# Down projection of a two-layer decoder trunk: 12 instead of 8 of 22 row tiles by seven products

## The chip, the cores and the metric

One core of a Trainium2 chip runs the whole program in one launch. The metric is the device time of that launch in microseconds; the host only lays arrays out. The kernel is written in Bass with the Tile framework: Tile assigns buffers, places semaphores and orders the instructions of every engine but PE, whose order is that of the program text.

Names of the engines as the profile has them: PE multiplies matrices (PEld is its loading of the stationary operand), DVE is the vector engine, ACT the scalar engine, POOL is GpSimd, which here only issues transfers, and SP issues the others.

## What is computed

The reference is two layers of a decoder trunk over 512 tokens of width 1024 in float32. Each layer has a gated feed-forward block, a mixer (a gated recurrence beside windowed attention) and a second gated feed-forward block, each between two normalisations. The change touches the feed-forward blocks alone:

```python
def swiglu(h, w_gate, w_up, w_down):
    return (jax.nn.silu(h @ w_gate) * (h @ w_up)) @ w_down

x = x + 0.5 * rms_norm(swiglu(h, w_ffn1_gate[l], w_ffn1_up[l], w_ffn1_down[l]), gn[1])
```

The inner width is 2816, so the down projection `... @ w_down` multiplies 512 x 2816 by 2816 x 1024. It is run four times: twice per layer, in two layers.

## The kernel before

**Precision.** Every float32 factor is split into hi (rounded to the format fp32r) and lo (the rest), and a product is three passes, hi x hi, hi x lo and lo x hi (`mm3`). A split is an ACT copy that makes hi and a DVE subtraction that makes lo (`split`, L401 and L402 for activations; L325 and L332, or L282 and L287, for weights). `split_dma` makes lo in another way: ACT makes hi (L411), ACT writes the negative of the source (L412), and a transfer issued by POOL adds the source to it (L413); DVE has no part in it.

**Tiles of the down projection.** The activations lie as 22 row tiles of 128 inner indices by 512 tokens, the list `src`. Each is the stationary operand, 128 tokens at a time; a half of the weight's columns (512) is the moving one. The result is `y[t][h]` in PSUM, for four token tiles t and two column halves h. A unit (j, h) is the pair of row tiles 2j and 2j + 1 for one column half; its weights are one item of 128 x 1024, and `both(j, h)` runs its 24 matmuls.

**Seven products.** For eight row tiles (8 to 15, `LEAD` = 8 and the next eight) the 2 x 2 block product of (two halves of the tokens, two groups of four rows) with (two groups of four rows, two column halves) is done in Winograd's form by seven instead of eight block products. `Late.sums` prepares the sums of the activations: x1 (the first block as it is), s for products 5 and 6, and t for products 3 and 7. `Stream.quarter` prepares those of the weights, of raw units and of `side` loads b12 and b22 that stay in SBUF. `quarters` runs the products in the order `ORDER` = p1, p6, p2, p7, p5, p4, p3, two weight items each, and adds them up on DVE (L790).

**Order of one projection before.** Four lead units of half 0 (rows 0 to 7), during which `Late.sums` runs for one row per unit and `ready` splits the rows `EARLY` = 4 ahead; then the seven products; then the units 8, 9 and 10 of half 0; `fetch` (the residual and the gains, to SBUF); three units of half 1; and the tail, the last four units of half 1 (`TAIL`), run one token tile after the other, with the normalisation of a finished token tile (`post`, `norm`) beside the matmuls of the next. The first block of the next stage is started in the tail (`pre.turn`). Ahead of the projection lies the loop of `sevenths`, one per row tile; the last one's silu and z (L895, L896) make row 21.

**Buffers and queues.** Nearly all activations of 128 x 512 share the tag "s" with 61 slots; a slot is taken by the first instruction that writes the tile and is free after the last one that uses it. Raw weight units have 4 slots (`W32`), hi and lo of weights 6 each (`WS`), and weight items are prepared `AHEAD` = 3 (`most`) items ahead of the one in use. "tt" has two slots, "m" one. `pin` keeps an instruction behind the one written before it on its engine; without it Tile may move an instruction forward when its inputs and its slot are there. PSUM has five tiles "acc" and three "aux". SP issues the loads in its order, POOL the adding transfers in its own.

Of the kernel before, what the change touches and what calls it, by code (L numbers as in the profile page):

```python
# [15 lines left out]
P = 128  # L16
# [22 lines left out]
LEAD = 8  # L39
ORDER = ("p1", "p6", "p2", "p7", "p5", "p4", "p3")  # L40
DMAS = ()
# [4 lines left out]
def trunk(ctx: ExitStack, tc: tile.TileContext, xin, wall, gains, lbT, hgain, sinks, c_dist, c_mask, c_ident, out):  # L46
# [109 lines left out]
    class Stream:  # L156
# [36 lines left out]
        def rows(self, kt, fast):  # L193
# [13 lines left out]

            j0, later = LEAD // 2 if fast else 0, []
            if fast:
                for j in range(j0):  # L210
                    unit(j, 0)

                u = self.n
                for q in range(2):
                    self.src[u + q] = pieces(j0 + q, 0)
                    self.src[u + 2 + q] = pieces(j0 + 2 + q, 0)
                self.side[u + 1] = [pieces(j0 + q, 1) for q in range(4)]
                for k in ORDER:
                    for q in range(2):
# [3 lines left out]
                self.t2 = [None, None]  # L223
                self.n += 4
                for j in range(j0):
                    later.append(j)
                j0 += 4
            for j in range(j0, kt // 2):
                unit(j, 0)
                later.append(j)  # L230
            for j in later:
                unit(j, 1)
            self.wall = u0 + kt

        def load(self, upto):
            while self.dma < min(upto, self.n):
# [10 lines left out]
                if u in self.side:  # L247
                    self.b12, self.b22 = [], []
                    for i, ps in enumerate(self.side[u]):
                        v = [big(), big()]  # L250
                        for c, a in ps:
                            nc.sync.dma_start(v[c.start // S][:, c.start % S : c.start % S + 2 * P], a)
                        (self.b22 if i > 1 else self.b12).append(v)

        def quarter(self, it):

            self.load(it.base + 4)
            q, h = it.q, (slice(0, S), slice(S, D))
            if it.kind in ("p1", "p2", "p5", "p4"):
                w = [self.raw[it.u][:, c] for c in h]  # L260
                if it.kind == "p4":
                    for c in range(2):
                        pin(nc.vector.tensor_tensor(w[c], w[c], self.t2[q][c], op=ALU.add))
            elif it.kind == "p6":

                t = sb.tile([P, D], F32, tag="tt", name=nm("tt"), bufs=2)
                self.t2[q] = w = [t[:, c] for c in h]
                for c in range(2):
                    t1 = self.raw[it.u][:, h[c]]
                    pin(nc.vector.tensor_tensor(t1, t1, self.b12[q][c], op=ALU.subtract))  # L270
                    pin(nc.vector.tensor_tensor(w[c], t1, self.b22[q][c], op=ALU.subtract))
            elif it.kind == "p3":
                w = self.b22[q]
            elif it.kind == "p7":

                w = self.b12[q]
                for c in range(2):
                    pin(nc.vector.tensor_tensor(w[c], w[c], self.b22[q][c], op=ALU.add))
            it.hi = sb.tile([P, D], F32R, tag="whi", name=nm("whi"), bufs=WS)
            it.lo = sb.tile([P, D], F32R, tag="wlo", name=nm("wlo"), bufs=WS)  # L280
            for c in range(2):
                nc.scalar.copy(it.hi[:, h[c]], w[c])  # L282
                if it.kind in DMAS:
                    nc.scalar.mul(it.lo[:, h[c]], w[c], -1.0)
                    nc.gpsimd.dma_start(it.lo[:, h[c]].bitcast(F32), w[c], accum_op=ALU.add)
                else:
                    nc.vector.tensor_tensor(it.lo[:, h[c]], w[c], it.hi[:, h[c]].bitcast(F32), op=ALU.subtract)  # L287
            self.done += 1
            self.flight += 1
            if it.kind in ("p5", "p4"):  # L290
                self.raw.pop(it.u)
                self.freed += 1
                self.load(self.freed + W32)
# [103 lines left out]
    def split(src, scale=None, to=None):  # L397

        hi, lo = to or (big(F32R), big(F32R))
        if scale is None:  # L400
            nc.scalar.copy(hi, src)  # L401
# [70 lines left out]
    class Quarters:  # L472
# [4 lines left out]
        def operand(self, n):  # L477
# [4 lines left out]
            return [[v[:, i, :] for v in x[k]] for k in range(4)]  # L482
# [127 lines left out]
    class Late(Quarters):  # L610


        def __init__(self, src, k0):
            self.src, self.k0 = src, k0
            self.x1, self.x56, self.x37, self.t = [], [], [], []
# [12 lines left out]
        def more(self, n):  # L628

            for i in range(len(self.x37), n):  # L630
                self.src[self.k0 + 4 + i] = split(self.src[self.k0 + 4 + i])
                self.x37.append(pair_split(self.t[i], split_dma))

        def raw(self, half, i):
            return [cut(self.src[self.k0 + 4 + k], HALF[half]) for k in range(4)] if i else self.x1

    def down(src, kt, l, n, nxt, fast):
# [8 lines left out]
        pre = Pre(*nxt) if nxt else None  # L646

        def ready(n):

            for i in range(min(n, kt)):  # L650
# [6 lines left out]
        def piece(b, t, h, j, i):  # L657
            st = cut(src[2 * j + i], slice(t * P, (t + 1) * P))
            mm3(y[t][h], st, [halves(w, i) for w in b[2:]], 2 * j + i == 0 and not (fast and h and t < 2), 2 * j + i == kt - 1)
# [20 lines left out]
        js = list(range(kt // 2))  # L680
        if fast:
            late = Late(src, LEAD)
            for j in range(LEAD // 2):
                ready(2 * j + EARLY)
                while len(late.x56) < min(4, 8 * (j + 1) / LEAD):
                    late.sums()
                both(j, 0)
            more = quarters(late, y)
            del js[LEAD // 2 : LEAD // 2 + 4]
        for j in js[LEAD // 2 if fast else 0 :]:  # L690
            ready(2 * j + 2 + EARLY)
            both(j, 0)
        if not fast:
            for t in range(TT):
                y[t][1] = aux() if t > 1 else acc()
        fetch()
        last = js[-TAIL:]
        for j in js[:-TAIL]:
            both(j, 1)

        warm = small([P, 1], "warm", 2)
        pin(nc.scalar.activation(out=warm, in_=src[last[0]][0][:, :1].bitcast(F32), func=AF.Sqrt, bias=eps_t, scale=0.0))
# [69 lines left out]
    def quarters(late, y):  # L772
# [3 lines left out]
        def product(n, o, start, stop=True):  # L776
            its = [ws.whole(), ws.whole()]
            for k in range(4):
                for t in range(2):
                    st = cut(late.operand(n)[k], slice(t * P, (t + 1) * P))  # L780
                    it = its[k // 2]
                    mv = [w.rearrange("p (m two c) -> p m two c", two=2, c=P)[:, :, k % 2, :] for w in (it.hi, it.lo)]
                    mm3(o[t], st, mv, start and k == 0, stop and k == 3)
# [12 lines left out]
        late.more(2)  # L796
        p = product(1, two(acc), True)
        p1, u2, u3, c12, c22 = (two(big) for _ in range(5))
        for t in range(2):
            nc.scalar.copy(p1[t], p[t])  # L800
        late.more(4)

# [649 lines left out]
```

## Time and profile before

| | before |
|---|---|
| median of 3 runs | 2100.99 us (2100.95 to 2102.06) |
| the profiled execution: its own time | 2100.66 us |
| the profiled execution: span | 2098.9 us |
| first matmul of the four fast down projections, in the span | 240.9, 935.1, 1279.3, 1973.2 us |

The page of the profile has the busy time of each engine and its share of the span first, then the span in 40 slices, then the chain of work that ended last by engine. A group line reads: line of the kernel, engine, operation, tiles out<-in, shape, count, then busy us and mean ns of one, then the idle time of the engine just before these instructions and what ended it. A line of the chain or of an engine's instructions in order of time reads: start in us, us, what, count. A line of windows reads: stretch, its length, busy us (and instructions) of PE, PEld, DVE, ACT and POOL, the granted clock, the busy share of the DMA engines, GB/s. Times that are given "after a lead's start" count from the first matmul of a down projection.

### The profile page before, as it was taken

Reading aid. Unit: us, or ns where it says so; the run is one execution under the profiler, and the core shown is the slowest. Engines: PE = TensorE matmul, PEld = TensorE weight load, DVE = VectorE, ACT = ScalarE, POOL = GpSimd, SP = SyncE. Lnnn points to the kernel's source line nnn. Section 1 sums busy time; section 2 is a strip of 40 time slices with the busy share of each in tenths; the row PEclk is TensorE's granted clock in tenths of the full one; section 3 lists DMA queues with packets and bytes.
Section 4 is the critical chain, followed back from the end, with each engine's and each line's share of the span. In section 5 each row is a group of like instructions: output and inputs, shape, how many; then the busy total and the mean of one; then the engine's idle time right before and its main releaser. Section 6 shows DMA issues by size and latency. Waiting matters only on the chain.

```text
span 2098.9 us, 35207 instructions
## 1 busy us (share of the span) xinstructions
PE 2090.3 (100%) x13549; PEld 1875.3 (89%) x13549; DVE 1550.5 (74%) x2705; ACT 1122.4 (53%) x1899; POOL 154.2 (7%) x188
## 2 busy tenths in 40 slices
PE   9999999999999999999999999999999999999998
PEld 8899988887888999998899998898778989999987
DVE  5877886766776777789587778767687758777884
ACT  6555564456454555556455556554653545555562
POOL 0011000000000011110001110000000000111000
PEclk9999999999999999999999999999999999999999
DMA  8577653312236357774447775632122563677651
GB/s 246 152 181 184 178 157 135 111 61 71 71 101 203 127 122 182 181 198 122 154 114 176 183 181 150 191 120 92 51 81 61 136 193 103 159 182 181 184 160 51
DMA packets 148071, 298.35 MB, mean 142 GB/s; under 512 B 16992, under 2 KB 74816, under 8 KB 147904
## 3 DMA queue, kind: packets, MB, share of 16 engines
q1 hardware_dynamic: 122416, 228.16, 33.2%
q0 software_dynamic: 25344, 67.91, 18.7%
q8 instruction: 106, 1.74, 0.3%
q14 instruction: 61, 0.50, 0.1%
q10 hardware_dynamic: 144, 0.05, 0.0%
HBM read 213.43 MB, written 14.73 MB: 109 GB/s over the span
## 4 chain that ended last, share of the span: by engine, by line
PE 88%; DMA 0%; DVE 0%; ACT 0%; SPq 0%; issue 0%; ACTq 0%
PE acc L115 64%; PE aux L115 22%; PE aux L125 1%; PE acc L125 1%; DMA wlo<-w 0%; DMA w<-wall 0%; SPq L241 0%; DVE s L402 0%; ACT whi L282 0%; DVE s L731 0%; ACT s L600 0%; DVE s L712 0%; DVE s L896 0%; DVE wlo L287 0%; ACT m L895 0%
## 5 line engine op out<-in xcount | busy, mean ns | idle before, releaser
L115 PE MATMUL acc<-s,whi 128*128 128x256 f32 (+1 forms) x4952 | 1059.3, 311 | 0.4 <-ACT whi L325 0.3
L115 PEld LDWEIGHTS acc<-s,whi 128*128 128x128 f32 x4952 | 808.0, 191 | 51.3 <-issue 3.2
L115 PE MATMUL acc<-s,wlo 128*128 128x256 f32 (+1 forms) x2476 | 766.6, 310 | 0.1
L115 PEld LDWEIGHTS acc<-s,wlo 128*128 128x128 f32 x2476 | 472.6, 191 | 25.0 <-DVE wlo L332 0.4
L325 ACT CAST whi<-w 128x1024 fp32r<-128x1024 f32 (+1 forms) x341 | 316.6, 948 | 237.6 <-PE acc L115 95.5
L115 PE MATMUL acc<-whi,s 128*128 128x512 f32 x1264 | 413.6, 393 | 0.1
L325 ACT CAST whi<-tt 128x1024 fp32r<-128x1024 f32 x154 | 161.4, 1048 | 326.5 <-DVE tt L319 184.2
L332 DVE TENSOR_TENSOR wlo<-w,whi 128x1024 fp32r<-128x1024 f32 (+1 forms) x181 | 218.3, 1215 | 151.4 <-ACT whi L325 149.6
L115 PEld LDWEIGHTS acc<-whi,s 128*128 128x128 f32 x1264 | 237.1, 188 | 54.7 <-ACT whi L325 1.6
L332 DVE TENSOR_TENSOR wlo<-tt,whi 128x1024 fp32r<-128x1024 f32 x154 | 188.1, 1221 | 98.8 <-ACT whi L325 98.7
L115 PE MATMUL acc<-wlo,s 128*128 128x512 f32 x632 | 246.4, 390 | 0.0
L115 PE MATMUL aux<-s,whi 128*128 128x256 f32 (+1 forms) x1248 | 230.4, 285 | 0.0
L330 POOL DMA_DIRECT2D wlo<-w x160 | 137.8, 863 | 1258.6 <-ACT wlo L329 704.9
L115 PE MATMUL aux<-whi,s 128*128 128x512 f32 x592 | 196.7, 390 | 0.0
L115 PEld LDWEIGHTS aux<-s,whi 128*128 128x128 f32 x1248 | 195.2, 192 | 1.1 <-issue 0.5
L115 PE MATMUL aux<-s,wlo 128*128 128x256 f32 (+1 forms) x624 | 177.5, 284 | 0.0
L115 PEld LDWEIGHTS acc<-wlo,s 128*128 128x128 f32 x632 | 118.7, 188 | 23.4
L115 PEld LDWEIGHTS aux<-whi,s 128*128 128x128 f32 x592 | 111.1, 188 | 22.8
L329 ACT ACTIVATE wlo<-w 128x1024 fp32r<-128x1024 f32 (+1 forms) x160 | 129.8, 844 | 0.0
L401 ACT CAST s<-s 128x512 fp32r<-128x512 f32 (+1 forms) x164 | 88.4, 580 | 71.5 <-DVE s L460 67.9
L115 PEld LDWEIGHTS aux<-s,wlo 128*128 128x128 f32 x624 | 119.8, 192 | 0.3
L115 PE MATMUL aux<-wlo,s 128*128 128x512 f32 x296 | 115.2, 389 | 0.0
(186 smaller groups left out, 2128.6 us busy)
## 6 DMA issues: line engine op xcount, KB each, us to landing
w<-wall SPq DMA_DIRECT2D x267, 512.0 KB, 3.7
wlo<-w POOLq DMA_DIRECT2D x83, 512.0 KB, 5.5
w<-wall SPq DMA_DIRECT2D x288, 128.0 KB, 3.3
wlo<-w POOLq DMA_DIRECT2D x77, 256.0 KB, 3.3
x_d<-s SPq DMA_DIRECT2D x48, 256.0 KB, 2.1
s<-x_d SPq DMA_DIRECT2D x48, 256.0 KB, 5.5
w<-wall SPq DMA_DIRECT2D x34, 256.0 KB, 3.0
s<-wall SPq DMA_DIRECT2D x64, 128.0 KB, 3.6
```

The source lines that it names most:

```text
L115: nc.tensor.matmul(o, lhsT, rhs, start=start, stop=stop)
L125: nc.tensor.transpose(o, src, ident)
L325: i = nc.scalar.copy(it.hi[:, c], w[:, c])
L329: nc.scalar.mul(it.lo[:, c], w[:, c], -1.0)
L330: nc.gpsimd.dma_start(it.lo[:, c].bitcast(F32), w[:, c], accum_op=ALU.add)
L332: nc.vector.tensor_tensor(it.lo[:, c], w[:, c], it.hi[:, c].bitcast(F32), op=ALU.subtract)
L401: nc.scalar.copy(hi, src)
```

## The change

`LEAD` goes and `SEVEN` = 12 comes: rows 0 to 11 are done by seven products, with groups of six rows instead of four, three weight items per product instead of two, and twelve instead of eight side tiles. Rows 12 to 21 are done plainly, in five units. The order of one projection is now: the five units 6 to 10 of half 0; the products in the order p1, p3, p7, p2, p6, p4, p5; one unit of half 1; the tail of four units.

- In the lead, the rows 16 to 21 are split at once, before its first unit, into pairs (`part`) that are used for half 0 and dropped; the ACT copies are pinned. The rows are split a second time for half 1, by `ready(kt)`, behind product 4. `early` splits rows 12 to 15 instead of 0 to 3.
- `Late.sums` runs for two rows after each of the first three units. x1's ACT copy is pinned, x37 is made at once by `split_dma`, and s is kept as it is. Behind product 7, `rest` splits rows 6 to 11 and `more` splits s, both by `split_dma`.
- The look-ahead on weight items goes 3, 2, 2, 3, 3 over the five units; weight copies traced in the lead are pinned.
- The sums of weights are formed differently: p7 makes b12 + b22 and, from it, t2 = raw - that; p6 uses t2 and adds it to b22 for p5; p4 adds t2 to its raw unit. All DVE operations of `quarter` are pinned.
- In PSUM, y[0] and y[1] of half 1 take "aux" before product 3, y[2] and y[3] of half 1 take "acc" after product 5. Products are taken up by DVE in five pairs of additions instead of four.
- `fetch` stands behind product 4.

```diff
-LEAD = 8
-ORDER = ("p1", "p6", "p2", "p7", "p5", "p4", "p3")
+SEVEN = 12
+ORDER = ("p1", "p3", "p7", "p2", "p6", "p4", "p5")
...
+                self.side[u + n - 1] = [pieces(n + q, 1) for q in range(n)], [pieces(q, 1) for q in range(n)]
                 for k in ORDER:
-                    for q in range(2):
-                        it = Item(k, u + q + (2 if k in ("p2", "p4") else 0), 4)
+                    for q in range(n):
+                        it = Item(k, u + q + (n if k in ("p2", "p4") else 0), 4)
...
+            elif it.kind == "p7":
                 w = self.b12[q]
+                sums(w, w, self.b22[q], ALU.add)
+            elif it.kind == "p6":
+                w = self.t2[q]
+            else:
+                w = raw
+                sums(w, w, self.t2[q], ALU.add)
...
+            if it.kind == "p7":
+                t = sb.tile([P, D], F32, tag="m" if q == 2 else "tt", name=nm("t2"), bufs=1 if q == 2 else 2)
+                self.t2.append([t[:, c] for c in h])
+                sums(self.t2[q], raw, w, ALU.subtract)
+            elif it.kind == "p6":
+                sums(self.b22[q], self.b22[q], w, ALU.add)
...
         def sums(self):
-            k = self.k0 + len(self.x56)
-            a = [self.src[i][:, c] for i in (k, k + 4) for c in HALF]
+            k = len(self.x1)
+            a = [self.src[i][:, c] for i in (k, k + self.n) for c in HALF]
             x = big(F32R, [P, 2, S // 2])
-            self.x1.append(split(a[0], to=(x[:, 0, :], x[:, 1, :])))
+            self.x1.append(split(a[0], to=(x[:, 0, :], x[:, 1, :]), hold=pin))
             s, t = quarter_sums(a[0], a[2], a[1], a[3], True)
-            self.x56.append(pair_split(s))
-            self.t.append(t)
+            self.s.append(s)
+            self.x37.append(pair_split(t, split_dma))
             self.src[k] = ()
+        def rest(self):
+            for k in range(self.n, 2 * self.n):
+                self.src[k] = split_dma(self.src[k])
+        def more(self):
+            self.x37 = None
+            while self.s:
+                self.x56.append(pair_split(self.s.pop(0), split_dma))
...
+            late = Late(src)
+            ws.pinned = True
+            for k in range(2 * js[0] + EARLY, kt):
+                part[k] = split(src[k], hold=pin)
+            for i, j in enumerate(js):
+                ws.most = (3, 2, 2, 3, 3)[i]
+                both(j, 0)
+                while len(late.x1) < min(late.n, 2 * i + 2):
                     late.sums()
+                for k in (2 * j, 2 * j + 1):
+                    part.pop(k, None)
+            ws.pinned = False
+            more = quarters(late, y, lambda: (ready(kt), fetch()))
...
+        p1, u3, c12, c22 = (two(big) for _ in range(4))
         for t in range(2):
             nc.scalar.copy(p1[t], p[t])
+        for t in range(2):
+            y[t][1] = aux()
+        product(3, [y[t][1] for t in (0, 1)], True, False)
+        p = product(7, two(acc), True)
+        late.rest()
+        late.more()
+        add(u3, p, p1)
+        product(2, [y[t][0] for t in (0, 1)], False)
+        p = product(6, two(acc), True)
+        add(c12, p, p1)
+        add(u3, p, u3)
+        product(4, [y[t][0] for t in (2, 3)], False)
+        fetch()
+        p = product(5, two(acc), True)
         add(c22, p, u3)
+        add(c12, p, c12)
```

More of the change, by code (lines that the diff above doesn't have):

```diff
@@ L646, in down @@
         pre = Pre(*nxt) if nxt else None
+        js = list(range(SEVEN // 2 if fast else 0, kt // 2))
+        part = {}
         def ready(n):
-            for i in range(min(n, kt)):
+            for i in range(2 * js[0], min(n, kt)):
                 if not isinstance(src[i], tuple):
@@ L657, in piece @@
         def piece(b, t, h, j, i):
[L658 to L659 removed]
+            k = 2 * j + i
+            st = cut(part.get(k) or src[k], slice(t * P, (t + 1) * P))
+            start, stop = k == 2 * js[0], k == kt - 1
+            if fast:
+                start, stop = start and (h == 0 or t > 1), stop and h == 1
+            mm3(y[t][h], st, [halves(w, i) for w in b[2:]], start, stop)
         xt = [[None] * 2 for _ in range(TT)]
@@ L770, in down, with quarters @@
         return pre
-    def quarters(late, y):
+    def quarters(late, y, fetch):
         def product(n, o, start, stop=True):
-            its = [ws.whole(), ws.whole()]
-            for k in range(4):
+            x = late.operand(n)
+            for k in range(late.n):
+                if k % 2 == 0:
+                    it = ws.whole()
+                mv = [w.rearrange("p (m two c) -> p m two c", two=2, c=P)[:, :, k % 2, :] for w in (it.hi, it.lo)]
                 for t in range(2):
[L780 to L783, printed above, removed]
+                    mm3(o[t], cut(x[k], slice(t * P, (t + 1) * P)), mv, start and k == 0, stop and k == late.n - 1)
                     ws.used((it, 1))
```

133 lines of the change are left out of this document (47 added, 86 removed).

## The prediction

> **What bounds the kernel now.** I read the page first: busy shares, granted clock and the chain that ended last.
>
> ```profile
> span 2098.9 us, 35207 instructions
> PE 2090.3 (100%) x13549; PEld 1875.3 (89%) x13549; DVE 1550.5 (74%) x2705; ACT 1122.4 (53%) x1899; POOL 154.2 (7%) x188
> PEclk9999999999999999999999999999999999999999
> PE 88%; DMA 0%; DVE 0%; ACT 0%; SPq 0%; issue 0%; ACTq 0%
> ```
>
> PE is busy for all but 8.6 us, at full clock, and nearly the whole chain is PE. A busy PE need not be a PE without waits, because matmul spans overlap, so I read the idle column of the groups that hold the down projections (moving operand whi or wlo, 512 columns), and then the chain in order of time across the second fast down projection.
>
> ```profile
> L115 PE MATMUL acc<-whi,s 128*128 128x512 f32 x1264 | 413.6, 393 | 0.1
> L115 PE MATMUL acc<-wlo,s 128*128 128x512 f32 x632 | 246.4, 390 | 0.0
> L115 PE MATMUL aux<-whi,s 128*128 128x512 f32 x592 | 196.7, 390 | 0.0
> L115 PE MATMUL aux<-wlo,s 128*128 128x512 f32 x296 | 115.2, 389 | 0.0
> ```
>
> ```profile
> 957.11 5.44 PE acc L115 x24
> 962.55 5.44 PE aux L115 x24
> 967.99 10.88 PE acc L115 x48
> 978.87 5.44 PE aux L115 x24
> ```
>
> Products 1, 6, 2 with 7, and 5 follow one another without a gap: 24 matmuls in 5.44 us, so one costs 0.2267 us of PE's time (the 390 ns of the groups are overlapping spans). Work taken off PE here shortens the run one for one, as long as the other engines keep ahead. Whether they can is read from the windows of that projection (its four lead units, its seven products, the three units after them):
>
> ```profile
> 935.10:956.90 21.80, 21.80 (x98) 18.05 (x97) 20.14 (x40) 9.30 (x19) 0.00 (x0) 1.00 0.55 167
> 957.10:995.20 38.10, 38.10 (x170) 31.55 (x169) 36.23 (x59) 26.45 (x46) 3.44 (x4) 1.00 0.48 123
> 995.20:1011.50 16.30, 16.30 (x73) 13.49 (x73) 9.01 (x11) 5.02 (x7) 0.00 (x0) 1.00 0.90 288
> ```
>
> The columns are PE, PEld, DVE, ACT, POOL. DVE is at 95% during the products and PE still never waits; behind them DVE has air. So PE is the bound and DVE is the engine to watch.
>
> **The change: what PE loses.** A row tile done plainly costs 4 token tiles x 2 column halves x 3 passes = 24 matmuls. Eight rows by seven products cost 7 x 4 x 2 x 3 = 168 instead of 192; twelve cost 7 x 6 x 2 x 3 = 252 instead of 288. Saved per projection: 36 instead of 24, so 12 more; four fast projections make 48. 48 x 0.2267 = 10.88 us. No other PE work is added. [...]
>
> **What the other engines gain to do.** Prices, from the second projection's DVE, ACT and POOL in order of time:
>
> ```profile
> 936.54 0.68 DVE L875 TENSOR_TENSOR m<-acc,s 128x512 f32<-128x512 f32 x1
> 937.15 2.61 DVE L287 TENSOR_TENSOR wlo<-w,whi 128x512 fp32r<-128x512 f32 x4
> 939.67 0.68 DVE L877 TENSOR_TENSOR s<-acc,m 128x512 f32<-128x512 f32 x1
> ...
> 942.16 0.69 DVE L896 SCALAR_TENSOR_TENSOR s<-m 128x512 f32<-128x512 f32 x1 [0.76 <-ACT m L895]
> ...
> 944.94 2.23 DVE L402 TENSOR_TENSOR s<-s,s 128x512 fp32r<-128x512 f32 x4 [0.28 <-ACT s L401]
> 947.09 0.42 DVE L459 TENSOR_TENSOR s<-s,s 128x256 f32<-128x256 f32 x1
> 947.43 0.42 DVE L463 TENSOR_TENSOR s<-s 128x256 f32<-128x256 f32 x1
> 947.76 0.42 DVE L460 SCALAR_TENSOR_TENSOR s<-s,s 128x256 f32<-128x256 f32 x1
> 948.21 0.43 DVE L462 TENSOR_TENSOR s<-s,s 128x256 f32<-128x256 f32 x1
> ...
> 964.28 2.49 DVE L287 TENSOR_TENSOR wlo<-w,whi 128x512 fp32r<-128x512 f32 x4
> ```
>
> ```profile
> 941.50 0.63 ACT L895 ACTIVATE m<-m 128x512 f32<-128x512 f32 x1 [2.47 <-DVE m L883]
> ...
> 958.58 0.62 ACT L411 CAST s<-s 128x512 fp32r<-128x512 f32 x1
> 959.10 0.63 ACT L412 ACTIVATE s<-s 128x512 fp32r<-128x512 f32 x1
> ...
> 963.54 2.18 ACT L282 CAST whi<-w 128x512 fp32r<-128x512 f32 x4
> ```
>
> Back to back, a 512-wide DVE operation costs 2.49 / 4 = 0.62 us, the four quarter sums of one row pair 1.55 us, a 512-wide ACT operation 2.18 / 4 = 0.55 us.
>
> Seven products: 21 weight items instead of 14, PE consuming one per 12 x 0.2267 = 2.72 us, 57.1 us in all. DVE: 42 lo halves, 24 half-row sums (p7 four per item, p6 two, p4 two), 10 PSUM adds and the 6 tail rows split a second time, 82 x 0.62 = 50.8 us, 89%. The same count for before is 28 + 16 + 8 + 4 row splits = 56 x 0.62 = 34.7 of 38.1 us, 91%, and that ran without a wait. Inside, only p7's items cost DVE more (6 x 0.62 = 3.72 us) than PE takes for one; six buffers of hi and lo let DVE run up to five items ahead, p1 and p3 cost it only 1.24 each, and three times 1.0 us of loss eats about one item of that lead. ACT: 42 copies, 24 operations for the DMA-made splits of `rest` and `more`, 2 + 6 others, 74 x 0.55 = 41 of 57.1 us. Cost taken: nothing.
>
> Lead: 5 units, 5 x 5.44 = 27.2 us. DVE: 6 row splits (3.7), 6 row sums with x1's half split (6 x 1.9 = 11.4, a 256-wide operation being 0.34), five weight items (6.1), and the last gate's chain (about 3): 24 of 27.2 us. Before: 20.14 of 21.80.
>
> The first rows that can be late are 16 and 17. Their ACT copies are pinned behind the last silu, which before ran at 941.50 (PE began the lead at 935.1), with the last z behind it at 942.16. Two p1 items (the four L287 at 937.15, 2.6 us) leave this place, since p1 is five units away now; one row's sums (1.9) may come in. So the silu ends some 6 to 7 us after the lead's start, row 16 has hi and lo 1.5 us later, at 8.5, and PE wants it at 10.9. Here before had a wait, in the first projection, where rows 4 and 5 stood behind the sums:
>
> ```profile
> 251.85 0.44 PE L115 MATMUL acc<-whi,s 128*128 128x512 f32 x1
> 252.13 0.40 PE L115 MATMUL acc<-wlo,s 128*128 128x512 f32 x1
> 252.60 0.74 PE L115 MATMUL acc<-whi,s 128*128 128x512 f32 x2
> ```
>
> The starts stand 0.28 and 0.47 apart instead of 0.227, and the last pair takes 0.74 instead of 0.61: 0.4 us, which the new order should give back (bounds 0 and 0.4; taken 0.4).
>
> **The tight place: slots.** Tile "s" has 61. At the lead's start 26 hold rows (22 rows, four of them as pairs), 12 the side tiles, 12 the tail pairs of `part`: 50. Each row of `sums` takes five and gives two back (row and t). So three rows fit, and the other three wait for tail pairs: two slots each at about 15.6, 16.3, 21.1, 21.8, 26.5 and 27.2 us after the start (PE's last use of rows 16 to 21). The t of a row is free when its POOL transfer has landed:
>
> ```profile
> 960.02 0.86 POOL L413 DMA_DIRECT2D s<-s  x1 [31.60 <-DVE w L270]
> s<-s POOLq DMA_DIRECT2D x16, 256.0 KB, 3.4
> ```
>
> The sixth row's x37 then gets its slots when the fifth's t lands, at about 25.8, or with row 20's pair at 26.5 at the latest. Behind it on ACT, pinned, stands p1's second weight item, and behind its copies DVE's pinned lo: 26.5 + 2 x 0.55 + 2 x 0.55 + 0.62 = 29.3 us; PE wants that item at 27.2 + 2.72 = 29.9. It fits by 0.6. Bounds: 0, and one more landing (3.4 - 0.6 = 2.8 per projection); it is nearer to 0, taken 0.1 per projection, 0.4. Product 3 wants that row's transfer at 35.4 and has it by 27.6 + 3.4 = 31.
>
> PSUM: after product 5, y[2] and y[3] of the second half take the acc tiles that c22 and c12 are added from. The third add ends 3 x 0.62 = 1.9 us after product 5, PE wants the tile after 12 matmuls, 2.72; if DVE has just begun a weight item (1.23 us, below), 0.4 is lost. Bounds 0 and 0.4 per projection, taken 0.1: 0.4 in all.
>
> `fetch` moves ahead of product 5 on SP and `ready(kt)` into the products; only one unit instead of three stands between the products and the tail. There DVE had this much air per unit of 5.44 us:
>
> ```profile
> 1029.00 1.23 DVE L332 TENSOR_TENSOR wlo<-w,whi 128x1024 fp32r<-128x1024 f32 x1 [4.21 <-ACT whi L325]
> ```
>
> Four adds and eight halves of `half(t, 0)`, 12 x 0.62 = 7.4 us, with two weight items, 2.4, fit into the 10.9 us up to the first `post`: nothing. Were they late, the first transposes, 16 us on, would be next. Side loads and weight loads only trade places on SP: 32 pieces of 128 KB go from w to s, the bytes stay.
>
> **Sum.** The profiled execution took 2100.66 us (span 2098.9 and 1.8 around it). 2100.66 - 10.88 - 0.4 + 0.4 + 0.4 = 2090.2; the median of the runs stands 0.3 above that execution, so 2090.5.
>
> **Rivals.** (1) The tight place gives way: p1's second item comes 1 to 1.8 us late in each projection. For it: 0.6 us of margin built on 61 counted slots; against it: row 20's pair bounds it. 4 to 7 us back: 2094.5 to 2097.5, say 2096.
>
> (2) DVE becomes the bound in the products: no lead is stored, p7's 1.0 us is lost three times in each projection, 12 us: 2102, no change. For it: 95% busy before; against it: p1 and p3 let DVE gain 1.5 us per item right before p7.
>
> (3) Slower: the raw rows that product 2 needs. `rest` makes their lo by ACT, ACT and a POOL transfer, and is written behind product 7; if slots let it begin only when product 7 gives up x37's twelve, product 2 waits 0.62 + 0.63 + 3.4 - 0.45 (lo is wanted third) = 4.2 us in each projection, 16.8 in all: 2106.5. It decides from 2.7 us per projection, and shows as slower from 3.8. For it: POOL issues go from 4 to 18 per projection. Against it: by my count five slots are free from 27.2 us and x1's six from 35.4, product 2 starts at 51.7. [...]
>
> **How the numbers follow.** Forecast 0.60 (2089.5 to 2092.5), rival (1) 0.15, (2) 0.09, (3) 0.16. About 0.2% (4.2 us) is what a measurement of this kernel tells from no change: faster 0.75, same 0.09, slower 0.16. The range runs from 2089.3 (no wait anywhere is 2100.99 - 10.88 - 0.4 = 2089.7) to 2099.5: it holds the forecast, rival (1) and a part of what lies between (1) and (2).
>
> **What would show it.** Matmuls 13549 to 13501, the 512-wide whi and wlo groups from 2784 to 2736; seven products in 57.1 us; POOL L413-like issues 16 to 72; DVE busy up by about 40 us, ACT by about 65, with PE's idle column unchanged. Wrong steps would be gaps between matmul starts at 29.9 us after a lead's start (slots), at 51.7 (`rest`), inside product 7 or 2 with DVE as releaser, or 2.7 us after product 5 (PSUM). More than 2.7 us of them per projection makes the prediction wrong.

## The result and the profile after

| | before | after |
|---|---|---|
| median of 6 runs each, side by side | 2101.1 us (2100.01 to 2102.06) | 2110.19 us (2109.45 to 2111.36) |
| the profiled execution: its own time | 2100.66 us | 2109.45 us |
| the profiled execution: span | 2098.9 us | 2107.5 us |
| ratio to before, 95% interval | | 1.0045 [1.0034, 1.0056] |

The change makes the kernel 0.45% slower, although the matmuls that were to go are gone. The page of after:

```profile
span 2107.5 us, 35599 instructions
PE 2087.7 (99%) x13501; PEld 1870.3 (89%) x13501; DVE 1588.2 (75%) x2801; ACT 1180.9 (56%) x2035; POOL 203.1 (10%) x244
```

48 matmuls fewer, DVE 37.7 us and ACT 58.5 us more (about 40 and 65 were forecast). But PE's busy time fell by 2.6 us only, and the span is now 19.8 us longer than it, against 8.6 before. The groups of the down projections (last two fields: idle time ahead of them, and what ended it) say where:

```profile
L114 PE MATMUL acc<-whi,s 128*128 128x512 f32 x1344 | 442.3, 396 | 9.8 <-ACT whi L274 9.8
L114 PE MATMUL acc<-wlo,s 128*128 128x512 f32 x672 | 264.4, 393 | 1.2 <-DVE wlo L277 1.2
```

All of it stands before p1's weights: L274 and L277 are the copy and the subtraction that make hi and lo of a quarter's item. PE in order of time at that place of the second fast projection (its lead starts at 937.5; the first column is the start, the second the length, the bracket the idle time before):

```profile
967.22 0.39 PE L114 MATMUL acc<-whi,s 128*128 128x512 f32 x1
970.05 0.49 PE L114 MATMUL acc<-whi,s 128*128 128x512 f32 x1 [2.45 <-ACT whi L274]
970.86 0.50 PE L114 MATMUL acc<-wlo,s 128*128 128x512 f32 x1 [0.31 <-DVE wlo L277]
971.20 0.97 PE L114 MATMUL acc<-whi,s 128*128 128x512 f32 x2
971.97 0.63 PE L114 MATMUL acc<-wlo,s 128*128 128x512 f32 x1
972.40 1.05 PE L114 MATMUL acc<-whi,s 128*128 128x512 f32 x2
```

The last matmul of p1's first item starts at 967.22; at 0.227 us each the next would start at 967.45, which is 29.9 us after the lead's start, the moment that the prediction named. It starts at 970.05: 2.6 us late, and the first one that reads lo is 0.58 later still. Behind that the matmuls go at 0.43 instead of 0.227 us (971.97 to 972.40). The windows of the same place (stretch, length, PE, PEld, DVE, ACT, POOL, granted clock, DMA share, GB/s):

```profile
970.00:975.00 5.00, 4.63 (x12) 3.46 (x13) 5.00 (x10) 4.16 (x9) 0.13 (x1) 0.66 0.31 54
975.00:980.00 5.00, 5.00 (x24) 4.12 (x23) 4.05 (x8) 3.28 (x7) 0.00 (x0) 1.00 0.02 5
```

The granted clock is 0.66 in the five us from 970 on, with 12 matmuls in them where 22 fit at 0.227 us each (0.6 us went to the wait for lo), 0.51 in the three from 971.2 on, and 1.00 again from 975 on. The third projection has the same wait without that (clock 1.00 from 1317 to 1322):

```profile
1316.81 0.50 PE L114 MATMUL acc<-whi,s 128*128 128x512 f32 x1 [2.45 <-ACT whi L274]
1317.62 0.50 PE L114 MATMUL acc<-wlo,s 128*128 128x512 f32 x1 [0.31 <-DVE wlo L277]
1317.96 0.62 PE L114 MATMUL acc<-whi,s 128*128 128x512 f32 x2
1318.42 0.40 PE L114 MATMUL acc<-wlo,s 128*128 128x512 f32 x1
```

**The account.** From a lead's first matmul to the first matmul of the next stage (in the fourth, behind which no stage follows, to the last transpose of the output), read from the starts, in us:

| projection | before | before less 12 x 0.2267 | after | lost | wait at 29.9 | slow clock |
|---|---|---|---|---|---|---|
| 1 | 116.48 | 113.76 | 118.33 | 4.57 | 3.19 | 1.69 |
| 2 | 116.06 | 113.34 | 118.31 | 4.97 | 3.19 | 1.71 |
| 3 | 116.16 | 113.44 | 116.90 | 3.46 | 3.19 | 0.11 |
| 4 | 121.20 | 118.48 | 123.64 | 5.16 | 3.19 | 1.74 |

18.2 us are lost in the projections, 12.8 in one wait repeated four times and 5.2 in the clock behind it; the two together leave 0.15 us of the sum unexplained. With 10.9 saved and some 1.3 lost in small pieces outside the projections, the span grows by 8.6 us.

**Why p1's second item is late.** ACT in order of time (L408 and L409 make x37 of a row, the L398 of 256 columns makes the next row's x1):

```profile
952.39 0.62 ACT L408 CAST s<-s 128x512 fp32r<-128x512 f32 x1 [1.34 <-DVE s L459]
...
955.21 0.62 ACT L408 CAST s<-s 128x512 fp32r<-128x512 f32 x1 [1.36 <-DVE s L459]
...
960.22 0.62 ACT L408 CAST s<-s 128x512 fp32r<-128x512 f32 x1 [3.56 <-DVE s L459]
...
965.09 0.62 ACT L408 CAST s<-s 128x512 fp32r<-128x512 f32 x1 [2.38 <-issue]
...
967.83 0.62 ACT L408 CAST s<-s 128x512 fp32r<-128x512 f32 x1 [1.28 <-DVE s L459]
968.35 0.62 ACT L409 ACTIVATE s<-s 128x512 fp32r<-128x512 f32 x1
968.88 2.16 ACT L274 CAST whi<-w 128x512 fp32r<-128x512 f32 x4
```

and DVE, at the sums of the third and the fourth row:

```profile
953.14 0.42 DVE L456 TENSOR_TENSOR s<-s,s 128x256 f32<-128x256 f32 x1 [0.83 <-PE aux L114]
...
958.58 0.43 DVE L460 TENSOR_TENSOR s<-s 128x256 f32<-128x256 f32 x1 [3.14 <-PE aux L114]
```

L456 and L460 read raw rows and write s and t; nothing that PE makes goes into them. What PE releases is a slot: 953.14 is 15.6 us after the lead's start, when PE is done with row 16, 958.58 is 21.1, when it is done with row 18. The two waits are 4.0 us of DVE's time. Between the fourth and the fifth row stand the copies and the lo of p1's first item. The fifth row's x37 comes at 965.09, 27.6 us after the start, as soon as DVE has made its sums, so no slot holds it up. The sixth follows at 30.3 (predicted: 26.5), and p1's second item, pinned, directly behind it at 31.4. Even without a wait for a slot a row takes 2.8 us (952.39 to 955.21), since ACT makes the next x1, DVE the sums from it, and ACT then x37: the two engines wait for each other in turn. And t is given back later than priced, because its transfer takes 4.8 us to land instead of 3.4 (last figure):

```profile
s<-s POOLq DMA_DIRECT2D x72, 256.0 KB, 4.8
```

### The profile page after: what moved, and what is told of

Same layout as the page of the kernel before. It is cut to its first block, busy times and chain, and to the rows that moved or that the text cites. A ratio compares the mean times of both kernels' runs of the same rounds, so it can differ in the third digit from the quotient of the medians.

```text
span 2107.5 us, 35599 instructions
## 1 busy us (share of the span) xinstructions
PE 2087.7 (99%) x13501; PEld 1870.3 (89%) x13501; DVE 1588.2 (75%) x2801; ACT 1180.9 (56%) x2035; POOL 203.1 (10%) x244
## 3 DMA queue, kind: packets, MB, share of 16 engines
q8 instruction: 106, 1.74, 0.3%
## 5 line engine op out<-in xcount | busy, mean ns | idle before, releaser
L114 PE MATMUL acc<-whi,s 128*128 128x512 f32 x1344 | 442.3, 396 | 9.8 <-ACT whi L274 9.8
L322 ACT CAST whi<-w 128x512 fp32r<-128x512 f32 (+1 forms) x325 | 299.6, 942 | 163.0 <-PE acc L114 107.5
L114 PEld LDWEIGHTS acc<-whi,s 128*128 128x128 f32 x1344 | 254.4, 189 | 69.4 <-ACT whi L274 11.5
L329 DVE TENSOR_TENSOR wlo<-w,whi 128x1024 fp32r<-128x1024 f32 (+1 forms) x165 | 199.8, 1215 | 89.6 <-ACT whi L322 88.9
L114 PE MATMUL acc<-wlo,s 128*128 128x512 f32 x672 | 264.4, 393 | 1.2 <-DVE wlo L277 1.2
L114 PE MATMUL aux<-whi,s 128*128 128x512 f32 x480 | 159.2, 390 | 0.0
L114 PEld LDWEIGHTS acc<-wlo,s 128*128 128x128 f32 x672 | 127.5, 190 | 27.5 <-DVE wlo L277 2.5
L114 PEld LDWEIGHTS aux<-whi,s 128*128 128x128 f32 x480 | 90.1, 188 | 18.6
L911 DVE SCALAR_TENSOR_TENSOR s<-m 128x512 f32<-128x512 f32 x69 | 47.8, 693 | 76.2 <-ACT m L910 75.7
L398 ACT CAST s<-s 128x512 fp32r<-128x512 f32 (+1 forms) x148 | 78.2, 563 | 47.2 <-DVE s L457 43.6
```

The costliest lines, as they stand in the source:

```text
L114: nc.tensor.matmul(o, lhsT, rhs, start=start, stop=stop)
L322: i = nc.scalar.copy(it.hi[:, c], w[:, c])
L329: nc.vector.tensor_tensor(it.lo[:, c], w[:, c], it.hi[:, c].bitcast(F32), op=ALU.subtract)
L398: hold(nc.scalar.copy(hi, src))
L911: nc.vector.scalar_tensor_tensor(z, m[:, 0:2, :], -1.0, m[:, 2:4, :], op0=ALU.mult, op1=ALU.mult)
```

## The experiments

The theory: slots. The row sums wait for slots that only the lead's own units free, and p1's second item stands pinned behind them. The rivals: the pins as such (the copies would be in time if Tile could move them); the order of the text (the item is simply written too late); and DVE (with twelve rows it has no air, so that a wait removed here comes back elsewhere). Where no interval is given there was one run. "At 30" means 30 us after a lead's start. The expectations, written before each run, name the kernels by number: e1 has the weight copies unpinned, e8 x1's copy unpinned, e2 the item written earlier, e4 one slot more, e3 b12 loaded later, e5 both e2 and e3; e6, e7, e9, e10 and e13 change e5, and e12 fills the wait.

### The pins

```diff
-            ws.pinned = True
+            ws.pinned = False
```

> Weight copies of the lead are not pinned on ACT. In the changed kernel PE waits 3.2 us in each projection for product 1's second weight item, and then runs some ten matmuls at half clock. Theory order (the item stands behind the last row sums by pins on ACT and DVE): ACT may make hi early, but DVE's lo stays pinned behind the sums of row 5, which ended 29.9 us after the lead's start; so the wait shrinks to about 1.3 us, and the time to about 2096. Theory load (ACT and DVE simply have too much to do in the lead): wait and time as in the changed kernel, 2110. Theory slots says nothing else than theory order here.

2119.1 us, which neither theory had. Free to move, the weight copies run ahead of the row splits on ACT, and PE waits for a row's hi, 1.9 us at 12.8; lo of p1's item is then 2.1 us late at 34.6:

```profile
952.90 0.50 PE L114 MATMUL acc<-whi,s 128*128 128x512 f32 x1 [1.75 <-ACT s L398]
...
974.70 0.50 PE L114 MATMUL acc<-wlo,s 128*128 128x512 f32 x1 [1.98 <-DVE wlo L277]
```

So the pins hold an order that is needed. Another pin, that of x1's copy, was taken off alone:

```diff
-            self.x1.append(split(a[0], to=(x[:, 0, :], x[:, 1, :]), hold=pin))
+            self.x1.append(split(a[0], to=(x[:, 0, :], x[:, 1, :])))
```

> The changed kernel with only x1's ACT copies unpinned. In it one row of sums took 2.8 us, ACT and DVE waiting for each other in turn (1.34 us of idle time on ACT, 0.9 on DVE), where the prediction counted 1.9. Theory chain (the pins of x1 make the row sums serial): rows follow one another in 1.9 us or less, the sixth ends at least 3 us earlier, the wait at 29.9 us shrinks from 3.2 to below 0.5, and the time is 2096 to 2102. Theory slots alone: rows 4 to 6 wait for slots as before, and the wait stays over 2 us.

2107.71 us, and the wait is what it was, as the theory of slots alone had it:

```profile
970.06 0.49 PE L114 MATMUL acc<-whi,s 128*128 128x512 f32 x1 [2.45 <-ACT whi L274]
```

The 2.5 us less than after lie in the clock: here the same wait was followed by a slow stretch in the fourth projection alone (clock 0.72 from 2010 to 2016; 1.00 behind the wait in the other three).

### The item written earlier

```diff
-                ws.most = (3, 2, 2, 3, 3)[i]
+                ws.most = (3, 3, 3, 3, 3)[i]
```

> Look-ahead of three weight items throughout the lead, instead of 3, 2, 2, 3, 3: product 1's second item is then written, and pinned, ahead of the last two row sums. Theory order: the gap at 29.9 us after the lead's start goes, and with it the half clock; the time is 2090 to 2092. Theory load: the work in the lead is the same, so the item or the sums are late all the same, and the time stays over 2104.

2105.64 us, 1.0017 [1.0007, 1.0027]. The wait of 3.2 us becomes one of 0.6 at 33.4, at full clock; waits of 0.3 to 1.2 come up at 61 to 71, and one of 1.0 at 91.8, which after did not have:

```profile
970.83 0.50 PE L114 MATMUL acc<-wlo,s 128*128 128x512 f32 x1 [0.31 <-DVE wlo L277]
...
1029.15 0.50 PE L114 MATMUL acc<-whi,s 128*128 128x512 f32 x1 [0.78 <-DVE s L724]
```

L724 is an addition of `half(t, 0)`, which frees a PSUM tile. So the place in the text bears on the first wait, as the theory of order had it, but the time stays where the theory of load had it: behind the first wait, waits for DVE and for POOL's transfers take part of the gain back.

### More free slots

First by one slot (`SLOTS` = 62):

> One slot more of the tag, 62 (63 do not fit into the memory). Theory slots: rows take their slots one step earlier, and the wait of 3.2 us shrinks by at least half, below 1.6 us per projection: 2096 to 2102. Theory load: 2110 as before.

2102.73 us. The wait shrinks from 3.2 to 1.7 us, at 31.0:

```profile
968.34 0.50 PE L114 MATMUL acc<-whi,s 128*128 128x512 f32 x1 [0.93 <-ACT whi L274]
...
969.14 0.50 PE L114 MATMUL acc<-wlo,s 128*128 128x512 f32 x1 [0.31 <-DVE wlo L277]
```

One slot of 61 is worth 1.5 us in each of the four projections, and nothing else was changed in the kernel: the wait hangs on the slots. It is a little less than the theory had (a wait below 1.6 us, 2096 to 2102). The projections take 116.82, 115.23, 115.51 and 120.37 us, but each stretch with a mixer became 0.9 us longer, which points to other choices of Tile there.

Then by six slots: the six side tiles of b12, first wanted by p7, are loaded when p3's first item is prepared. In the second projection SP issues them from 19.4 to 31.0 us after the lead's start; in after it issued all twelve side tiles from 3.9 to 18.5.

```diff
-                    self.b22, self.b12, self.t2 = [], [], []
-                    for b, side in zip((self.b22, self.b12), self.side[u]):
...
+                    self.t2 = []
+                    self.b22 = self.beside(self.side[u][0])
+                    self.held = self.side[u][1]
...
+            if it.kind == "p3" and q == 0:
+                self.b12 = self.beside(self.held)
```

> The six side tiles b12, which only product 7 uses, are loaded when product 3's first item is prepared instead of before the lead; order and pins stay. Theory slots (the last row sums are late because the 61 slots of the tag are full, and the pinned item behind them with them): the sixth row's sums end before 24 us after the lead's start instead of at 30, the gap at 29.9 goes, 2090 to 2092. Theory load: the sums are as late as before, 2108 to 2110. If b12 now comes too late, a new gap stands at product 7, 43.5 us after the lead's start.

2103.49 us, 1.0008 [0.9998, 1.0017]. In the first three projections 0.9, 0.45 and 0.5 us are left at 30, less than with one slot more; in the fourth it is 1.7, as with one slot more. But a wait of 1.0 near 91 is there as in the kernel with the item earlier:

```profile
1027.07 0.50 PE L114 MATMUL acc<-whi,s 128*128 128x512 f32 x1 [0.86 <-DVE s L731]
```

The expectation that the sixth row's sums would end before 24 fell: in the second projection they ended at 27.5 instead of 30.3. There, as in the first and the third, no row waits for PE to free a slot any more (in the fourth one waits 1.4 us), but the rows still take 2.8 us each, with p1's first item between the fourth and the fifth. So of the 3.2 us some 2.3 to 2.7 are the slots, and the rest is the pace of the rows and the place in the text.

### Both together

```diff
-                ws.most = (3, 2, 2, 3, 3)[i]
+                ws.most = (3, 3, 3, 3, 3)[i]
```

on top of the later b12:

> e2 and e3 together: look-ahead three throughout and b12 loaded later. In each alone the wait at 29.9 us after the lead's start was gone or below 0.6 us, but a wait of 1.0 us stood 90 to 92 us after the lead's start, with DVE's addition of half(t, 0) as its releaser, and a few of 0.3 to 0.6 in the products. Theory order and slots: no wait is left before 60 us. Theory DVE behind (that DVE has no air from 60 us on, so that everything PE gains before shows up as a wait there): the wait near 91 us stays at 1 us or grows, and the time is 2100 to 2103.

2095.81 us (6 runs, 2092.91 to 2098.17), before beside it 2101.61: **0.9974 [0.9961, 0.9986]**, faster than both kernels, and better than the 2100 to 2103 of the theory that DVE is behind. In the first three projections nothing waits before 60; in the fourth 0.6 us are left. The projections take 114.54, 114.87, 113.67 and 120.35 us, 4.4 us in all above the third column of the account. The wait near 90 is 0.3 to 0.4 us in three projections and gone in the third. In the second one it is the longest that is left:

```profile
1023.37 0.50 PE L114 MATMUL acc<-whi,s 128*128 128x512 f32 x1 [0.24 <-DVE s L731]
```

How full DVE is there is seen in the windows from 72 to 95 us after a lead's start, of before, after and this kernel (third figure behind the length: DVE):

```profile
1007.10:1030.10 23.00, 23.00 (x103) 19.06 (x102) 11.05 (x14) 8.31 (x15) 0.00 (x0) 1.00 0.48 167
```

```profile
1009.50:1032.50 23.00, 23.00 (x103) 19.02 (x103) 22.67 (x33) 16.11 (x25) 0.00 (x0) 1.00 0.62 194
```

```profile
1005.90:1028.90 23.00, 22.75 (x99) 18.15 (x98) 21.88 (x31) 16.78 (x27) 0.00 (x0) 1.00 0.66 216
```

DVE had 12 of 23 us free here in before, and has 0.3 to 1.1 now. A full DVE alone does not make the wait, since after has none here. The next experiments take work away from that stretch, or move it.

### The late splits, moved and done another way

`more`, six splits of s, was written one split after each row of product 2 instead of all behind product 7, on top of the combined version, with 61 and with 62 slots:

```diff
+    def product(n, o, start, stop=True, each=lambda: None):
...
+                each()
...
-        late.more()
-        product(2, [y[t][0] for t in (0, 1)], False)
+        product(2, [y[t][0] for t in (0, 1)], False, True, late.more)
```

> e5, and the six splits of `more` are written one after each row of product 2 instead of in one piece ahead of it. In e3 ACT did them in a row, 6.2 us, while DVE stood idle for 3.5 us waiting for the weight copies behind them, and DVE then had no pause until the first unit of half 1. Theory DVE behind: the idle time of DVE near 57 us shrinks, the wait near 91 us falls below 0.4, and the time is 2 to 6 us below e5's. If the wait near 91 us comes from PSUM's order alone (the tile that PE takes is the one that half(t, 0) frees, wherever DVE stands), it stays at 1 us and the time with it. A new wait at product 6 (60 us) would show that the splits now come too late.

> e6 with 62 slots. Theory slots: whatever is left of the waits before 60 us shrinks. e4 ran the mixers 0.9 us slower each than the changed kernel, which the extra slot brings here too: e6 less what is left of its waits before 60 us, plus 1.8 us.

2112.08 us, 1.0051 [1.0036, 1.0066], and 2111.03 us, 1.0046 [1.0031, 1.0061]: misses. Tile still let ACT make the six in a row, only later, and product 6 waits for POOL's transfers, with 61 slots:

```profile
1008.97 1.01 PE L114 MATMUL acc<-whi,s 128*128 128x512 f32 x2 [2.93 <-DMA s<-s]
```

The second split of the tail's rows (`ready(kt)` behind product 4) was left to the last unit and the tail, again in the combined version:

```diff
-            more = quarters(late, y, lambda: (ready(kt), fetch()))
+            more = quarters(late, y, fetch)
```

> e5 with the second split of the tail rows back where the kernel before had its last row splits: rows 16 and 17 ahead of the first unit of half 1, 18 to 21 behind it, instead of all six ahead of product 5. Theory DVE behind (DVE runs without a pause from 72 to 95 us after the lead's start, and PE waits 0.4 us near 89 for the addition of half(t, 0)): the work is the same and comes nearer to its use, so the wait near 89 goes, and one of 1 to 3 us appears in the tail, from 91 us on, with a row split as its releaser: 2097 to 2106. If DVE is not behind, the time is e5's, 2095 to 2096, or less.

2105.47 us, 10 us above the combined version. The wait near 90 is gone, and PE waits for these rows instead:

```profile
1035.15 0.73 PE L114 MATMUL aux<-whi,s 128*128 128x512 f32 x2 [0.77 <-DVE s L406]
```

The expectation held, and the early place of these splits is the better one. Then the same splits in the combined version by `split_dma`, which takes them off DVE:

```diff
-                    src[i] = split(src[i])
+                    src[i] = (split_dma if fast and n == kt else split)(src[i])
```

> e5 with the second split of the tail rows made by ACT and POOL (`split_dma`) instead of ACT and DVE: 3.7 us less on DVE per projection, 3.3 us more on ACT. Theory DVE behind: the wait near 89 us goes, 2092 to 2094.5. If ACT was as short of time as DVE there, its weight copies come late, and the time is e5's or up to 3 us more.

2114.97 us, 1.0064 [1.0051, 1.0076], outside both expectations. Again the wait near 90 is gone, and in the first three projections a larger one stands at 113, before the transposes of the next block:

```profile
1053.79 1.54 PE L124 MATMUL acc<-ident,s 128*128 128x128 f32 x6 [5.32 <-DVE s L761]
```

```profile
1038.29 1.06 ACT L329 CAST whi<-w 128x1024 fp32r<-128x1024 f32 x1 [7.17 <-DMA w<-wall]
```

ACT stood 7.17 us for a weight load in the tail, with the squares of the normalisation (`post`) queued behind that copy.

### PSUM freed earlier

The two additions of `half(t, 0)` for t = 0 and 1 were written directly behind product 4, pinned, on top of the combined version (and left out where they stood):

```diff
+        for t in range(2):
+            pin(nc.vector.tensor_tensor(p1[t], y[t][0], p1[t], op=ALU.add))
```

> e5 with two DVE additions moved: half(t, 0) of the token tiles 0 and 1, which free the PSUM tiles that PE then takes for y[2] and y[3] of half 1, stand right behind product 4 instead of behind the second row splits and four weight items. No work is added. Theory PSUM behind DVE (what is left of e5's waits, 0.4 us near 89 in three of the four projections, is these two additions standing late in DVE's queue): that wait goes, in all four, and the time is 0.5 to 2 us below e5's, 2093.5 to 2095.5. If the tile that PE waits for is freed by product 5's own additions, which DVE reaches later still, the wait stays or grows to 1 us or more.

2107.83 us, 1.0031 [1.0019, 1.0044], a miss. The wait near 89 is gone in all four projections, and the last one takes 119.08 instead of 120.35 us. But the other three now wait 3.3 us at 111, before the transposes of the next block:

```profile
1048.75 1.65 PE L124 MATMUL acc<-ident,s 128*128 128x128 f32 x11 [3.26 <-DVE s L762]
```

PE is at the transposes 1.2 us sooner than in the combined version (107.5 instead of 108.7), and DVE has the scaled tile that they read (L762 here, L761 there) 2 us later. DVE in order of time, of this kernel (lead at 937.75) and of the combined version (lead at 933.88):

```profile
1045.07 0.68 DVE L732 TENSOR_TENSOR s<-acc,s 128x512 f32<-128x512 f32 x1
1045.67 0.20 DVE L609 TENSOR_SCALAR rt<-ss 128x1 f32<-128x1 f32 x2
1046.87 1.22 DVE L336 TENSOR_TENSOR wlo<-w,whi 128x1024 fp32r<-128x1024 f32 x1 [1.00 <-ACT whi L329]
...
1048.20 0.88 DVE L762 TENSOR_SCALAR s<-s,rt 128x512 f32<-128x512 f32 x2
```

```profile
1041.22 0.21 DVE L609 TENSOR_SCALAR rt<-ss 128x1 f32<-128x1 f32 x2
1041.42 0.69 DVE L731 TENSOR_TENSOR s<-acc,s 128x512 f32<-128x512 f32 x1
...
1042.41 0.88 DVE L761 TENSOR_SCALAR s<-s,rt 128x512 f32<-128x512 f32 x2
...
1043.87 1.22 DVE L336 TENSOR_TENSOR wlo<-w,whi 128x1024 fp32r<-128x1024 f32 x1
```

An addition has come ahead of the root's scale (L609), and a weight's lo ahead of the scaling: 110.5 us after the lead's start instead of 108.5. So the PSUM tile is the cause of the wait near 90, since freeing it sooner removes the wait. That this did not pay is put down to DVE's order into the tail, which came out differently; this is read from the trace and was not tested.

### The clock behind the wait

PE was given something to do in the wait: 14 unused matmuls of 512 columns between p1's first and second item.

```diff
+                if n == 1 and k == 1:
+                    junk = aux()
+                    for _ in range(14):
+                        mm(junk, x[k][0][:, :P], mv[0], True, True)
```

> The changed kernel with 14 matmuls of 512 columns, whose result nobody reads, between product 1's first and second weight item: 14 x 0.227 = 3.2 us, as long as PE waits there. Theory clock gate (the ten matmuls that take 0.427 instead of 0.227 us behind that wait in three of the four projections are slow because PE had stood still): with PE kept busy none is slow, and 56 matmuls more make the kernel 5 to 6 us faster, 2104 to 2106. If they are slow for another reason (weights that come at the pace of ACT and DVE), the time stays at 2109 to 2111.

2113.52 us, 1.0059 [1.0044, 1.0075]. No wait is left at 30 and no slow matmul, with windows at full clock:

```profile
965.00:970.00 5.00, 5.00 (x24) 4.14 (x23) 4.04 (x11) 1.45 (x3) 0.86 (x1) 1.00 0.30 52
970.00:975.00 5.00, 5.00 (x23) 3.94 (x22) 3.27 (x7) 4.96 (x10) 0.86 (x1) 1.00 0.62 108
```

Fed through the wait, PE keeps its clock, in all four projections; the mean granted clock is 0.999 in each of the four runs, and 0.994 to 0.996 in the six of after. That link is shown. The time was a miss: 14 x 0.227 = 3.2 us were spent in each projection to save 3.2 of waiting and, in three of them, 1.7 of slow clock, and new waits came up from 65 on, the longest, 1.0 us, at 93, where after had none:

```profile
1033.02 0.50 PE L114 MATMUL acc<-whi,s 128*128 128x512 f32 x1 [0.84 <-DVE s L724]
```

## Why the prediction was wrong

**Right.** 48 matmuls at 0.2267 us are off PE. Rows 16 and 17 are in time, and the first projection has its 0.4 us back: it lost 4.57 with 4.88 of wait and slow clock in it. DVE keeps up in the products: from their start at 964.70 on, at the rate of the sum (50.8 us predicted in 57.1, plus the wait),

```profile
964.70:1026.70 62.00, 59.24 (x253) 48.31 (x252) 51.78 (x84) 45.68 (x82) 12.12 (x14) 0.97 0.60 137
```

it was busy 51.78 us, and no product after p1 waits more than 0.2 us. So rivals (2), DVE, and (3), `rest` late for product 2, did not happen, and the seven products really cost the 252 matmuls.

**The step that failed** is "The tight place: slots", which ended "It fits by 0.6 ... nearer to 0, taken 0.1 per projection". The place, the moment (29.9) and the engine chain were right. The size was 3.2 us, above even the upper bound of 2.8. Three of its terms were off. (a) The count: "three rows fit", but the third row already waited at 15.6. By the count 57 of 61 slots were taken then (50, three for each of two rows, x1 of the third). Two of the four that are missing may be the t tiles of the first two rows, which the count took as given back: their transfers were issued at 951.05 and 953.84, and with 4.8 us to land neither was there at 953.14. That is argued; which tiles hold the other two was not found, and the count also gives the side tiles their slots from the lead's start, while SP issued the last of them at 18.5. (b) A landing was priced at 3.4 us, from 16 transfers; with 72 the median is 4.8. No row waits for a landing in this trace, so that this added to the 3.2 us is not shown. (c) A row was priced at 1.9 us, as DVE's work alone; it takes 2.8 with ACT and DVE in turn, and p1's first item stands between the fourth row and the fifth. So the sixth row's x37 came at 30.3, and not with row 20's pair at 26.5, as the bound had it. With b12 later the shares are seen: without the waits for slots the 3.2 us fall to 0.45 to 0.9.

**Rival (1)** was this very mechanism, at 0.15 and at "1 to 1.8 us". At 3.19 it would have given back 12.8 us and no gain at all; at 0.6 of margin on 61 counted slots it deserved both more chance and a wider price.

**A term that was missing** is the clock: the sum priced a wait at its length, and so put the slow clock behind it at nothing. Here 3.2 us cost 4.9 in three projections of four, and these 5.2 us are what turns the result from even to plainly slower.

**PSUM and `half(t, 0)`.** In after the wait 2.7 us behind product 5 did not come. In five of the other kernels (the copies unpinned, the item earlier, b12 later, both, the wait filled) it came, 0.3 to 1.0 us long, and the tile was freed by an addition of `half(t, 0)` (L724, L731), not by those of c22 and c12 as the prediction had it. That PE comes early is not enough for it: with 62 slots PE is 1.4 to 3.1 us earlier than in after and does not wait, and with the wait filled PE is no earlier in the third projection and does wait. What differs is how many splits stand ahead of the second addition in DVE's order. Here are that addition and PE's first matmul into the tile that it frees, in the third projection, of after (lead at 1284.26; the second of PE's two matmuls) and with the wait filled (lead at 1286.60):

```profile
1374.07 0.69 DVE L724 TENSOR_TENSOR s<-acc,s 128x512 f32<-128x512 f32 x1
1375.99 0.61 PE L114 MATMUL acc<-whi,s 128*128 128x512 f32 x2
```

```profile
1379.07 0.69 DVE L724 TENSOR_TENSOR s<-acc,s 128x512 f32<-128x512 f32 x1
1379.81 0.50 PE L114 MATMUL acc<-whi,s 128*128 128x512 f32 x1 [0.82 <-DVE s L724]
```

In after the addition ends 90.5 us after the lead's start, and PE takes the tile at 91.95. In the other kernel three more splits stand ahead of it, it ends at 93.2, and PE follows at once. Why Tile ordered DVE differently is open. "Fit ... nothing" for this work was wrong too: it counted what DVE has to do in 10.9 us, without what stood in its queue from before, and the windows show 22.67 of 23 us busy. The combined version, at 2095.8, does not reach the forecast of 2090.5, and 4.4 us of the 5.3 lie inside the projections; 1.2 of them are this wait in three projections, 0.7 a wait at 33 in the fourth, and the rest is spread in pieces of 0.2 us and less.

**Open**: which tiles hold the other slots, why the stretches outside the projections are 0.3 to 0.4 us longer, and whether another order of DVE's queue from 72 us on would free the rest.

## What to carry to other kernels

When a change puts more tiles through a pool of fixed size, count the slots at each moment with the transfers that have not landed still holding theirs, and when the count fits by less than one landing or one row's time, price the wait as likely. An instruction that is pinned behind the last user of such a pool inherits its wait, so write what the bound engine needs next ahead of it, or load later what fills the pool without being used yet; here only both together gave a gain. Before work is taken off the bound engine, look in windows for the stretch in which the next engine has least air: there the order of that engine's queue decides whether a gain is kept, and it can come out differently in each version of the kernel.

## What the hardware showed that was not expected

A wait of PE cost more than its length in some projections and not in others. 2.6 and 0.6 us of idleness, 0.2 us of work between them, were followed in three of the four projections of after by six or seven matmuls 0.40 to 0.43 us apart, 1.7 us lost in each, and in the second by a granted clock of 0.66 over five us; behind the same wait in the third projection the clock was 1.00, as it was in three projections with x1's pin off, where the fourth had 0.72 over six us. Behind the waits of 1.1 and 0.6 us with one slot more the matmuls stood 0.23 us apart in all four. With the late splits spread and 61 slots, PE stood 3.1 us until 1008.97, in product 6 of the second projection, and the granted clock was 0.57 from 1009 to 1013. How long a wait must be to slow the clock is not shown. A transfer that adds from SBUF to SBUF took 3.4 us from issue to landing, at the median, when 16 were issued by POOL, and 4.8 when 72 were, 18 of them in each projection.
